# Two-layer hybrid trunk on one core: stores issued by ScalarE, and the modulation product on quarters of TensorE's columns

## Chip, core and metric

The kernel runs on one core of a Trainium2 chip. The metric is the device time of one execution in microseconds. Before the change it was 3992.55 us, the median of 3 runs (3977.74 to 3996.63).

## What is computed

A trunk of two layers over 2304 tokens (256 of context, then 2048 latent) of width 1024, in float32. Of the reference, this matters here:

```python
for i in range(DEPTH):                       # two layers
    sh_l, sc_l, gt_l = ada_modulation(c, w_mod[i], b_mod[i])       # silu(c) @ w_mod + b_mod, split in 3
    sh_c, sc_c, gt_c = ada_modulation(c_ctx, w_mod[i], b_mod[i])
    ml = layer_norm(xl) * (1.0 + sc_l) + sh_l
    mc = layer_norm(xc) * (1.0 + sc_c) + sh_c
    ... = jnp.split(ml @ w_in[i], PROJ_SPLITS, axis=-1)            # one wide projection, three branches
    oa_c, oa_l = gdn_branch(...)     # bidirectional gated DeltaNet, chunks of 64
    ob_c, ob_l = na_branch(...)      # neighbourhood attention
    oc_c, oc_l = gla_branch(...)     # bidirectional gated linear attention
    y_l = concatenate([norm_gate(oa_l), ob_l * silu(z), norm_gate(oc_l)]) @ w_out[i]
    xl = layer_norm(ALPHA * xl + gt_l * y_l) * ln_g[i] + ln_b[i]
```

The modulation product has two rows alone (the conditioning of the latent tokens and of the context) against a 1024 x 3072 matrix in each layer.

## The kernel before

The tokens lie in 18 tiles of 128, and in 6 blocks of 384. The order of every engine's instructions is made when the program is built, by a scheduler that puts whatever is ready first on its engine by priority and by a planned time; the order that results is then fixed, each engine takes its own list in order, and waits on semaphores. All DMAs before are issued by SP, in one list, so an issue that waits holds back all those behind it.

The stages of a layer, with the lines that matter here:

- `stage_mod` (line 90) makes the modulation in parts of 512 columns: parts 0 to 3 are shift and scale, 4 and 5 the gate of the layer's end. For each part it loads the bias `b` (line 98), loads eight 128 x 512 slices `w` of the matrix (line 102), multiplies each by the two columns `e.cc[:, k]` into one PSUM tile `p` of 2 x 512 (line 104), adds the bias (line 105), and transposes the two rows into columns of `modT` (lines 111, 112), or stores them to `GT` (line 107). Layer 0 makes parts 0 to 3 at the very start; parts 4 and 5 of layer 0 and 0 to 3 of layer 1 lie in the first convolution run of layer 0, parts 4 and 5 of layer 1 in that of layer 1. A float32 product shows as two passes in the trace: 96 products are 192 matmuls.
- `stage_p1` (line 161) and `modulate` (line 136) load `x`, normalise it, transpose it (line 153), let ScalarE scale and shift it into `m` (line 156) and store it to `M` in DRAM (line 158). In layer 0's last stage `modulate` is called again for each tile, for layer 1.
- `Dense.block` loads `M` (line 237), splits it into two halves `mm` and stores these to `MS` (line 240); later runs load `MS` (line 234). `Dense.run` multiplies with `w_in` (line 190, the bulk of TensorE's work); its weights are loaded as `raw` (line 220).
- `Gla` consumes the callbacks `cb_q`, `cb_r`, `cb_v` (stores at lines 352, 360, 371) and stores a forward output per tile (`OC`, line 523).
- `Gdn.conv` makes convolutions on VectorE; `head_prep` stores q and k (line 665, last written by VectorE) and `kvt` (line 693, last written by ScalarE) to `KK`. `gates` stores `GR` and `GE` (line 747). `Gdn.step` is the recurrence over 18 tiles in two directions; it stores its output to `OA` (line 1040): the first of the two directions to reach a tile copies it with ScalarE (line 1039), the second loads what is there and adds with VectorE (lines 1035, 1036).
- `Natten.cb_v` stores `Vb` (line 1095). `Out` ends the layer.

Of the kernel before, what the change touches and what calls it, by code (L numbers as in the profile page):

```python
# [89 lines left out]
def stage_mod(e, pool, ps, tag, tt, bufs, w_mod, b_mod, modT, GT, parts, step):  # L90


    nc = e.nc
    w4 = w_mod.rearrange("(k p) n -> p k n", p=128)
    for n in parts:
        s = slice(512 * n, 512 * n + 512)
        b = pool.tile([2, 512], F32, tag="bm", name="b", bufs=2)
        nc.sync.dma_start(b, b_mod[s].partition_broadcast(2))
        p = ps.tile([2, 512], F32, tag=tag, name="p")
        for k in range(0, KD, step):  # L100
            w = pool.tile([128, step, 512], F32, tag="wm", name="w", bufs=bufs)
            nc.sync.dma_start(w, w4[:, k:k + step, s])
            for j in range(step):
                nc.tensor.matmul(p, e.cc[:, k + j], w[:, j], start=k + j == 0, stop=k + j == KD - 1)  # L104
        nc.vector.tensor_tensor(b, b, p, op=ALU.add)
        if n >= 4:
            nc.sync.dma_start(GT[:, 512 * (n - 4):512 * (n - 3)], b)
            continue
        pt = ps.tile([128, 4, 2], F32, tag=tt, name="pt")
        for j in range(4):  # L110
            nc.tensor.transpose(pt[:, j], b[:, j * 128:(j + 1) * 128], e.ident[0:2, 0:2])
        nc.vector.tensor_scalar(modT[:, 4 * n:4 * n + 4], pt, float(n >= 2), None, op0=ALU.add)
# [25 lines left out]
def modulate(e, P, ps, x, mu, r, t, modT, M, xn=None):  # L138
# [19 lines left out]
    nc.sync.dma_start(M[b][:, :, o:o + 128], m)  # L158
# [169 lines left out]
class Gla:  # L328
# [20 lines left out]
    def cb_q(self, P):  # L349
        def f(p, b):  # L350
            self.e.nc.scalar.activation(self.qk0[:, 1], p, AF.Copy, scale=32 ** -0.5)
            self.e.nc.sync.dma_start(self.QK[b], self.qk0)
        return f

    def cb_r(self, P, ps):
        def f(p, b):
            e, nc = self.e, self.e.nc
            r = P.tile([48, BLK], F32, tag="r48", name="r48", bufs=1)
            nc.scalar.copy(r, p)
            nc.sync.dma_start(self.RC[b], r[0:32])  # L360
            pt = ps.tile([128, TPB, 48], F32, tag="dn", name="pt")
            for t in range(TPB):
                nc.tensor.transpose(pt[:, t], r[:, t * 128:(t + 1) * 128], e.ident[0:48, 0:48])
            nc.vector.tensor_copy(e.ab[:, b * TPB:(b + 1) * TPB], pt[:, :, 32:48])
        return f

    def cb_v(self, P):
        def f(p, t):
            v = P.tile([128, 256], F32, tag="bv", name="cv")
            self.e.nc.scalar.copy(v, p[:, 0:256])  # L370
            self.e.nc.sync.dma_start(self.V[t * 128:(t + 1) * 128], v)
# [137 lines left out]
    def chunk(self, c, i, A, E, et, V):  # L509
        e, nc, P, ps = self.e, self.e.nc, self.p, self.ps  # L510
        t0 = i * 128
        if c >= self.first:
# [10 lines left out]
            nc.sync.dma_start(self.OC[c], o1)  # L523
# [52 lines left out]
class Gdn:  # L576
# [84 lines left out]
    def head_prep(self, P, psd, h, b, kq, vb):  # L661
# [31 lines left out]
        nc.sync.dma_start(self.KK[c0:c1, :, h, 2:4].rearrange("c p i t -> p c (i t)"), kvt.rearrange("p c i t -> p c (i t)"))  # L693

    def gates(self, P, ps):
# [34 lines left out]
        for d in range(2):  # L730
# [15 lines left out]
            for x, y in enumerate((self.GR, self.GE)):  # L746
                nc.sync.dma_start(y[d], gr[:, x])
# [230 lines left out]
    def step(self, s, d, c, n):  # L978
# [55 lines left out]
        if c in s.seen:  # L1034
            nc.sync.dma_start(ot, self.OA[c, :, h0:h0 + 2])
            nc.vector.tensor_tensor(ot, ot, po, op=ALU.add)
        else:
            s.seen.add(c)
            nc.scalar.copy(ot, po)
        nc.sync.dma_start(self.OA[c, :, h0:h0 + 2], ot)  # L1040
# [3 lines left out]
class Natten:  # L1044
# [44 lines left out]
    def cb_v(self, P):  # L1089
        nc = self.e.nc  # L1090

        def f(p, t):
            v = P.tile([128, 256], F32, tag="bv", name="bv")
            nc.scalar.copy(v, p[:, 0:256])
            nc.sync.dma_start(self.V[t * 128:(t + 1) * 128], v)
# [313 lines left out]
def layer(e, i, L, layers, xsrc, xdst):  # L1409
# [5 lines left out]
    with ExitStack() as lx:  # L1415
# [8 lines left out]
        if L == 0:  # L1424
            with ExitStack() as c:
# [3 lines left out]
                for n in (range(2), range(2, 4)):  # L1429
                    stage_mod(e, P, ps, "pa", "pm", 11, i["w_mod"][0], i["b_mod"][0], layers[0].modT, GT, n, 1)  # L1430
                    next(p1, None)
# [10 lines left out]
        with ExitStack() as gx:  # L1442
            with ExitStack() as dx:
                psd = pool(dx, "psd", 2, space=PSUM)
                dn = Dense(e, dx, psd, w, M)
                with ExitStack() as r:
# [15 lines left out]
                    with ExitStack() as c:  # L1462
                        ps = pool(c, "psr", 2, space=PSUM)
                        P, W = pool(c, "cv"), pool(c, "wa", side="right")
                        with ExitStack() as c1:
# [4 lines left out]
                            for j, n in ((L, range(4, 6)), (L + 1, range(4))):  # L1470
                                if j < DEPTH:
                                    stage_mod(e, P1, ps, "dn", "dn", 4, i["w_mod"][j], i["b_mod"][j], layers[j].modT, layers[j].GT, n, 1)
# [64 lines left out]
```

## Time and profile before

| | |
|---|---|
| median of 3 runs | 3992.55 us |
| the profiled execution | 3995.01 us, of which the span of instructions is 3992.9 us |
| TensorE busy | 3626.0 us (91%) |
| VectorE, ScalarE, GpSimd busy | 2521.8 us (63%), 1660.0 us (42%), 810.2 us (20%) |
| DMA | 787.57 MB, all but 4.9 MB of it on one queue; 63.6% of the 16 engines' time |
| mean granted TensorE clock | 0.913 of full speed |

Busy time of TensorE is modelled and includes stalls inside a stream, so the table says which engine is used most, not what ends the program last. For that the profile follows a chain back from the last instruction to whatever released each one. Issuing a DMA is not counted as busy time of the engine that issues it; it shows as instructions of a queue (SPq is SP's), with a duration of their own.

### The profile page before, as it was taken

Reading aid. Unit: us, or ns where it says so; the run is one execution under the profiler, and the core shown is the slowest. Engines: PE = TensorE matmul, PEld = TensorE weight load, DVE = VectorE, ACT = ScalarE, POOL = GpSimd, SP = SyncE. Lnnn points to the kernel's source line nnn. Section 1 sums busy time; section 2 is a strip of 40 time slices with the busy share of each in tenths; the row PEclk is TensorE's granted clock in tenths of the full one; section 3 lists DMA queues with packets and bytes.
Section 4 is the critical chain, followed back from the end, with each engine's and each line's share of the span. In section 5 each row is a group of like instructions: output and inputs, shape, how many; then the busy total and the mean of one; then the engine's idle time right before and its main releaser. Section 6 shows DMA issues by size and latency. Waiting matters only on the chain.

```text
span 3992.9 us, 77074 instructions
## 1 busy us (share of the span) xinstructions
PE 3626.0 (91%) x27262; PEld 3113.1 (78%) x27262; DVE 2521.8 (63%) x7471; ACT 1660.0 (42%) x4387; POOL 810.2 (20%) x1182
## 2 busy tenths in 40 slices
PE   7999998899989999897898999999999898989788
PEld 3777787579977888896676778887998788879676
DVE  5465462668975676356875556527798766753587
ACT  4533231335433454446545333213454244545342
POOL 0121111210101332221232211112111132331133
PEclk8988988899999998898898888899999998988899
DMA  9843435876687876666647443268776887775753
GB/s 312 280 147 105 133 112 169 245 232 201 205 276 219 246 229 189 187 196 214 203 132 232 152 147 115 100 210 251 215 232 201 285 228 205 228 217 150 219 160 111
DMA packets 756088, 787.57 MB, mean 197 GB/s; under 512 B 190207, under 2 KB 665207, under 8 KB 755703
## 3 DMA queue, kind: packets, MB, share of 16 engines
q1 hardware_dynamic: 755702, 782.64, 63.6%
q8 instruction: 216, 3.54, 0.4%
q14 instruction: 170, 1.38, 0.1%
HBM read 548.41 MB, written 234.03 MB: 196 GB/s over the span
## 4 chain that ended last, share of the span: by engine, by line
PE 55%; DMA 19%; DVE 16%; ACT 4%; issue 3%; SPq 2%; POOL 0%; DVEq 0%; ACTq 0%; POOLq 0%
PE p L190 29%; DMA mm<-MS 3%; PE p L1245 3%; DMA gb<-GR 2%; PE p L104 2%; DMA kk<-KK 2%; DMA raw<-in_w_in 1%; PE py L190 1%; PE po L1030 1%; PE pk L999 1%; PE pv L1010 1%; DMA oa<-OA 1%; PE pd L1017 1%; PE pt L1236 1%; DVE y L1374 1%
## 5 line engine op out<-in xcount | busy, mean ns | idle before, releaser
L190 PE MATMUL p<-mm,wh 128*128 128x384 f32 (+1 forms) x3648 | 1004.0, 354 | 67.2 <-DMA mm<-MS 21.4
L190 PEld LDWEIGHTS p<-mm,wh 128*128 128x128 f32 (+1 forms) x3648 | 667.8, 192 | 133.7 <-DMA mm<-MS 36.9
L190 PE MATMUL p<-mm,wl 128*128 128x384 f32 (+1 forms) x1824 | 635.1, 350 | 1.8 <-DVE wl L182 1.8
L190 PE MATMUL p<-wh,mm 128*128 128x512 f32 (+1 forms) x1696 | 570.5, 409 | 14.5 <-DMA mm<-MS 4.9
L190 PEld LDWEIGHTS p<-wh,mm 128*128 128x128 f32 x1696 | 329.1, 197 | 92.0 <-DMA mm<-MS 8.4
L649 DVE SCALAR_TENSOR_TENSOR acc<-pre,cw,acc 128x384 f32<-128x384 f32 (+1 forms) x576 | 351.8, 629 | 39.2 <-ACT acc L647 35.8
L190 PEld LDWEIGHTS p<-mm,wl 128*128 128x128 f32 (+1 forms) x1824 | 348.9, 191 | 22.8 <-issue 14.6
L190 PE MATMUL p<-wl,mm 128*128 128x512 f32 (+1 forms) x848 | 341.5, 403 | 4.3 <-DVE wl L182 4.3
L190 PE MATMUL py<-wh,mh 128*128 128x512 f32 x544 | 221.7, 410 | 17.1 <-ACT mh L1360 13.2
L190 PE MATMUL py<-wh,ml 128*128 128x512 f32 x544 | 213.9, 405 | 8.7 <-DVE ml L1361 8.7
L190 PE MATMUL py<-wl,mh 128*128 128x512 f32 x544 | 217.8, 402 | 0.0
L190 PEld LDWEIGHTS p<-wl,mm 128*128 128x128 f32 x848 | 166.5, 196 | 38.5 <-DVE wl L182 4.8
L992 POOL TENSOR_TENSOR kd<-kk,eD 128x256 f32<-128x256 f32 x144 | 90.4, 628 | 476.4 <-DMA kk<-KK 225.6
L1224 ACT ACTIVATE w<-w,mn 128x696 f32<-128x696 f32 (+2 forms) x136 | 112.9, 830 | 143.9 <-DVE mn L1221 142.6
L1383 POOL TENSOR_TENSOR y<-y,g 128x1024 f32<-128x1024 f32 x32 | 77.5, 2423 | 416.0 <-ACT y L1382 416.0
L639 POOL COPY pre<-pre 128x4 f32<-128x4 f32 x120 | 75.0, 627 | 416.4 <-DVE acc L649 244.1
L913 DVE TENSOR_TENSOR tmp<-M 96x30 f32<-96x30 f32 (+4 forms) x360 | 127.1, 353 | 27.7 <-issue 11.3
L1245 PE MATMUL p<-v,wl 120*128 120x64 f32 (+1 forms) x960 | 141.1, 286 | 0.0
L853 DVE SCALAR_TENSOR_TENSOR gb<-gb,Gt,mats 128x128 f32<-128x128 f32 x288 | 86.7, 358 | 83.0 <-DMA gb<-GR 82.8
L1261 DVE SCALAR_TENSOR_TENSOR zt<-zt,p 128x256 f32<-128x256 f32 (+1 forms) x102 | 51.4, 506 | 138.8 <-ACT zt L1260 131.9
L190 PEld LDWEIGHTS py<-wh,mh 128*128 128x128 f32 x544 | 106.4, 196 | 41.4 <-ACT mh L1360 16.1
L914 DVE TENSOR_TENSOR M<-M,tmp 96x30 f32<-96x30 f32 (+4 forms) x360 | 130.4, 362 | 6.1
(307 smaller groups left out, 8021.8 us busy)
## 6 DMA issues: line engine op xcount, KB each, us to landing
mm<-MS SPq DMA_DIRECT2D x384, 384.0 KB
kk<-KK SPq DMA_DIRECT2D x144, 512.0 KB
MS<-mm SPq DMA_DIRECT2D x96, 384.0 KB
raw<-in_w_in SPq DMA_DIRECT2D x104, 256.0 KB
w<-in_w_mod SPq DMA_DIRECT2D x96, 256.0 KB
M<-m SPq DMA_DIRECT2D x36, 512.0 KB
mm<-M SPq DMA_DIRECT2D x96, 192.0 KB
KK<-kq SPq DMA_DIRECT2D x96, 192.0 KB
```

What stands on the lines that cost most here:

```text
L104: nc.tensor.matmul(p, e.cc[:, k + j], w[:, j], start=k + j == 0, stop=k + j == KD - 1)
L190: e.nc.tensor.matmul(p, x(k), y(k), start=n == 0, stop=n == 3 * KD - 1)
L639: nc.gpsimd.tensor_copy(pre[:, 0:4], pre[:, m:m + 4])
L649: nc.vector.scalar_tensor_tensor(acc[:, :n], pre[:, k:k + n], w(kind, k), acc[:, :n], op0=ALU.mult, op1=ALU.add)
L853: nc.vector.scalar_tensor_tensor(E[:, d, h], gb[:, d, h], self.G[:, d, c, h0 + h:h0 + h + 1], e.mats[:, 1 + d], op0=ALU.subtract, op1=ALU.min)
L913: nc.vector.tensor_tensor(tv, col, row, op=ALU.mult)
L914: nc.vector.tensor_tensor(o, o, tv, op=ALU.add)
L992: nc.gpsimd.tensor_tensor(kd, kv[:, :, 0], self.eD[:, d, c, h0:h0 + 2].unsqueeze(2).to_broadcast([128, 2, 128]), op=ALU.mult)
L1224: nc.scalar.activation(w[:, a, 0:256 + nk], w[:, a, 0:256 + nk], AF.Exp, bias=m[:, a:a + 1], scale=-1.0, accum_out=sm[:, a:a + 1])
L1245: nc.tensor.matmul(p[:, a], l, r, start=j == 0, stop=j == len(parts) - 1)
L1261: nc.vector.scalar_tensor_tensor(th[:, :n], th[:, :n], 1.0, z, op0=ALU.add, op1=ALU.mult)
L1383: eng.tensor_tensor(y[:, s], y[:, s], self.g[:, 0, s], op=ALU.mult)
```

## The change

Two edits. **Stores**: where ScalarE is the last to write what a store sends out, the store is issued by ScalarE (`nc.scalar.dma_start`) instead of SP. These are 36 of `M`, 12 of `QKc`, 12 of `RC`, 36 of `Vc`, 34 of `OC`, 48 of `KK<-kvt`, 8 of `GR` and `GE`, 36 of `Vb`, and 68 of the 136 of `OA` (those after the copy): 290 DMAs. **Modulation**: up to four parts are made together. Part i takes partitions 32i and 32i+1 of the PSUM tile, and its product stands on the i-th quarter of the array's columns. One load brings two parts' slices (128 x 1024, 512 KB), so 48 loads take the place of 96; the bias is added part by part, and the transposes take all 128 partitions. `b` is zeroed first, on GpSimd. At the start 6 buffers of 512 KB take the place of 11 of 256 KB, in the convolution runs 2 in place of 4. The first block's `x` and its statistics are now asked for ahead of the modulation.

```diff
-    for n in parts:
-        s = slice(512 * n, 512 * n + 512)
...
-        p = ps.tile([2, 512], F32, tag=tag, name="p")
-        for k in range(0, KD, step):
-            w = pool.tile([128, step, 512], F32, tag="wm", name="w", bufs=bufs)
-            nc.sync.dma_start(w, w4[:, k:k + step, s])
-            for j in range(step):
-                nc.tensor.matmul(p, e.cc[:, k + j], w[:, j], start=k + j == 0, stop=k + j == KD - 1)
-        nc.vector.tensor_tensor(b, b, p, op=ALU.add)
...
+    n0, n = parts[0], len(parts)
+    b = pool.tile([128, 512], F32, tag="bm", name="b", bufs=1)
+    nc.gpsimd.memset(b, 0.0)
+    for i, x in enumerate(parts):
+        nc.sync.dma_start(b[32 * i:32 * i + 2], b_mod[512 * x:512 * x + 512].partition_broadcast(2))
+    p = ps.tile([128, 512], F32, tag=tag, name="p")
+    for k in range(KD):
+        for i0 in range(0, n, 2):
+            w = pool.tile([128, 2, 512], F32, tag="wm", name="w", bufs=bufs)
+            nc.sync.dma_start(w, w4[:, k, 512 * (n0 + i0):512 * (n0 + i0) + 1024].rearrange("p (i c) -> p i c", i=2))
+            for i in range(i0, i0 + 2):
+                nc.tensor.matmul(p[32 * i:32 * i + 2], e.cc[:, k], w[:, i - i0], start=k == 0, stop=k == KD - 1, tile_position=(0, 32 * i))
+    for i in range(n):
+        r = slice(32 * i, 32 * i + 2)
+        nc.vector.tensor_tensor(b[r], b[r], p[r], op=ALU.add)
...
+    for j in range(4):
+        nc.tensor.transpose(pt[:, j], b[:, j * 128:(j + 1) * 128], e.ident)
...
-    nc.sync.dma_start(M[b][:, :, o:o + 128], m)
+    nc.scalar.dma_start(M[b][:, :, o:o + 128], m)
...
-            nc.sync.dma_start(self.OC[c], o1)
+            nc.scalar.dma_start(self.OC[c], o1)
...
-        nc.sync.dma_start(self.KK[c0:c1, :, h, 2:4].rearrange("c p i t -> p c (i t)"), kvt.rearrange("p c i t -> p c (i t)"))
+        nc.scalar.dma_start(self.KK[c0:c1, :, h, 2:4].rearrange("c p i t -> p c (i t)"), kvt.rearrange("p c i t -> p c (i t)"))
...
             nc.vector.tensor_tensor(ot, ot, po, op=ALU.add)
+            nc.sync.dma_start(self.OA[c, :, h0:h0 + 2], ot)
         else:
             s.seen.add(c)
             nc.scalar.copy(ot, po)
-        nc.sync.dma_start(self.OA[c, :, h0:h0 + 2], ot)
+            nc.scalar.dma_start(self.OA[c, :, h0:h0 + 2], ot)
...
-                for n in (range(2), range(2, 4)):
-                    stage_mod(e, P, ps, "pa", "pm", 11, i["w_mod"][0], i["b_mod"][0], layers[0].modT, GT, n, 1)
-                    next(p1, None)
+                next(p1)
+                stage_mod(e, P, ps, "pa", "pm", 6, i["w_mod"][0], i["b_mod"][0], layers[0].modT, GT, range(4))
+                next(p1, None)
...
-                                    stage_mod(e, P1, ps, "dn", "dn", 4, i["w_mod"][j], i["b_mod"][j], layers[j].modT, layers[j].GT, n, 1)
+                                    stage_mod(e, P1, ps, "dn", "dn", 2, i["w_mod"][j], i["b_mod"][j], layers[j].modT, layers[j].GT, n)
```

The same one-word edit as in `modulate` is made in `cb_q`, `cb_r`, both `cb_v` and `gates`. The scheduler makes a new order from this, on every engine. Three places show what it moved. Lines of the new program are 8 higher in its first part (198 is the old 190, 164 the old 156), and 9 higher in the layer's code.

The first is TensorE in the first convolution run of layer 0, where modulation products (`p<-w,cc`) stand among the dense products. Before:

```order
L104 MATMUL p<-w,cc 2x512
L190 MATMUL p<-mm,wl 128x384
L190 MATMUL p<-mm,wh 128x384
L104 MATMUL p<-w,cc 2x512
L190 MATMUL p<-mm,wh 128x384
L190 MATMUL p<-mm,wl 128x384
L190 MATMUL p<-mm,wh 128x384
L104 MATMUL p<-w,cc 2x512
```

And now:

```order
L198 MATMUL p<-mm,wl 128x384
L198 MATMUL p<-mm,wh 128x384 x2
L107 MATMUL p<-w,cc 2x512 x2
L198 MATMUL p<-mm,wl 128x384
L198 MATMUL p<-mm,wh 128x384 x2
L198 MATMUL p<-mm,wl 128x384
L198 MATMUL p<-mm,wh 128x384 x2
L198 MATMUL p<-mm,wl 128x384
L107 MATMUL p<-w,cc 2x512 x2
```

Single products became pairs on two quarters of the columns; the 48 products of this run stand in 22 places in place of 38. At the program's start all 32 stand together, ahead of the first transpose.

The second is SP just after the last modulation load at the start, where the first block of `M` is stored and loaded back. Before:

```order
L158 DMA M_70<-m 1024x1x128
L220 DMA raw<-in_w_in 128x256 x2
L158 DMA M_70<-m 1024x1x128
L167 DMA x<-in_x 128x1024
L220 DMA raw<-in_w_in 128x256 x2
L167 DMA x<-in_x 128x1024
L220 DMA raw<-in_w_in 128x256 x2
L158 DMA M_70<-m 1024x1x128
L167 DMA x<-in_x 128x1024
L220 DMA raw<-in_w_in 128x256 x2
L158 DMA M_71<-m 1024x1x128
L237 DMA mm<-M_70 128x384 x7
```

And now:

```order
L105 DMA w<-in_w_mod 128x1024 x2
L228 DMA raw<-in_w_in 128x256 x9
L175 DMA x<-in_x 128x1024
L228 DMA raw<-in_w_in 128x256 x3
L228 DMA raw<-in_w_in 128x4x128
L175 DMA x<-in_x 128x1024
L228 DMA raw<-in_w_in 128x4x128 x3
L175 DMA x<-in_x 128x1024
L228 DMA raw<-in_w_in 128x4x128 x2
L175 DMA x<-in_x 128x1024
L228 DMA raw<-in_w_in 128x4x128
L245 DMA mm<-M_70 128x384 x8
```

The stores of `M` are gone from SP's list, and the loads that stood between them follow one another.

The third is ScalarE at the same place, as it is now (before, its list held activations and casts alone):

```order
L164 ACTIVATE m<-p,modT_77 128x128 x4
L166 DMA M_70<-m 1024x1x128
L187 CAST wh<-raw 128x256
L164 ACTIVATE m<-p,modT_77 128x128 x4
L187 CAST wh<-raw 128x256
L164 ACTIVATE m<-p,modT_77 128x128
L187 CAST wh<-raw 128x256
L164 ACTIVATE m<-p,modT_77 128x128 x3
L166 DMA M_70<-m 1024x1x128
L187 CAST wh<-raw 128x512
```

A store stands directly behind the last activation of its tile, and the casts and activations of the next tile behind the store.

## Rows read from the trace of the kernel before

**Rows 1.** The page: busy time by engine, and the chain's shares by engine.

```profile
PE 3626.0 (91%) x27262; PEld 3113.1 (78%) x27262; DVE 2521.8 (63%) x7471; ACT 1660.0 (42%) x4387; POOL 810.2 (20%) x1182
...
PE 55%; DMA 19%; DVE 16%; ACT 4%; issue 3%; SPq 2%; POOL 0%; DVEq 0%; ACTq 0%; POOLq 0%
```

**Rows 2.** Chain by line in stretches 0:45, 40:90, 735:870 and 2690:2780.

```profile
by line: PE p L104 47.2%; DMA w<-in_w_mod 34.5%; SPq L1275 4.0%; SPq L1277 2.6%; issue 1.6%; DVE b L105 1.5%; SPq L98 1.4%; DVE lnst L122 1.3%; SPq L83 1.3%; SPq L82 0.9%; SPq L571 0.9%; SPq L569 0.9%; PE pt L111 0.8%
...
by line: DMA M<-m 24.3%; DMA x<-in_x 18.8%; ACT m L156 11.7%; PE p L190 9.7%; DVE lnst L122 8.8%; PE p L104 8.6%; issue 5.7%; ACT mm L179 5.3%; DVE wl L182 1.5%; DVE b L105 1.3%; PE p L153 1.3%; DVE lnmv L123 1.1%; SPq L220 1.0%; PE pt L363
...
by line: PE p L190 50.7%; PE p L104 29.0%; DMA mm<-MS 13.5%; SPq L1118 1.7%; PE pq L670 1.5%; PE p L676 0.9%; PE p L690 0.8%; PE pt L111 0.5%; SPq L102 0.4%; SPq L234 0.4%; issue 0.3%; SPq L98 0.2%
...
by line: DVE acc L649 24.0%; DMA raw<-in_w_in 20.1%; DMA db<-in_dt_bias 6.8%; DMA mm<-MS 6.2%; issue 6.0%; DVE wl L182 5.0%; DVE kq L654 4.0%; ACT wh L179 3.5%; DVE s L712 2.7%; SPq L234 2.6%; ACT acc L647 2.1%; SPq L1118 2.0%; DVE vb L654 
```

**Rows 3.** Windows, line 104 alone: length, PE, PEld, granted clock, DMA share, GB/s.

```profile
0.00:45.00 45.00, 31.38 (x64) 4.85 (x64) 1.00 0.94 307
735.00:870.00 135.00, 47.35 (x96) 4.99 (x96) 1.00 0.89 260
2690.00:2780.00 90.00, 16.68 (x32) 1.81 (x32) 0.98 0.86 254
```

**Rows 4.** Waits of SP's queue: line, releaser: us in total, times, longest.

```profile
SPq L234 <- PE p L190: 179.7, 156, 12.8
...
SPq L693 <- ACT kvt L692: 77.0, 24, 8.2
...
SPq L523 <- ACT kd L529: 43.8, 17, 5.6
...
SPq L523 <- ACT o L522: 40.9, 10, 15.3
...
SPq L352 <- ACT cqk L351: 30.9, 7, 7.9
...
SPq L360 <- ACT r L359: 19.9, 6, 11.1
...
SPq L158 <- ACT m L156: 16.0, 8, 3.3
```

**Rows 5.** Timeline of PE: a modulation product (two passes) between dense ones.

```profile
842.82 1.02 PE L104 MATMUL p<-w,cc 128*2 128x512 f32 x2
843.77 0.62 PE L190 MATMUL p<-mm,wh 128*128 128x384 f32 x2
```

**Rows 6.** Timeline of PE: eight products on quarters of the columns (16 passes).

```profile
552.74 0.51 PE L190 MATMUL p<-mm,wh 128*128 128x384 f32 x2
553.18 0.43 PE L533 MATMUL pS<-v,kd 128*32 128x64 f32 x16
553.54 0.44 PE L190 MATMUL p<-mm,wl 128*128 128x384 f32 x1
```

**Rows 7.** Timeline of DVE: the last part's bias and its write to modT.

```profile
43.92 0.67 DVE L105 TENSOR_TENSOR b<-b,p 2x512 f32<-2x512 f32 x1 [2.06 <-PE p L104]
...
45.73 0.14 DVE L112 TENSOR_SCALAR modT<-pt 128x8 f32<-128x8 f32 x1
```

**Rows 8.** Chain in order of time: two landings of M; who waits for line 158.

```profile
63.36 5.25 DMA M<-m
...
74.27 6.89 DMA M<-m
...
  ACT m L156: 9.4, 8
```

**Rows 9.** Issue durations on SP (ns, min/median/max) at three lines.

```profile
L158 SPq DMA_DIRECT2D M<-m x36: 513/528/1105, 49.5 to 2154.4; - x36
...
L693 SPq DMA_DIRECT2D KK<-kvt x48: 359/366/1673, 794.5 to 3124.0; - x48
...
L1040 SPq DMA_DIRECT2D OA<-o x136: 319/382/1523, 1282.6 to 3745.3; - x136
```

**Rows 10.** Window 45:85, all engines: PE, PEld, DVE, ACT, POOL, clock, DMA.

```profile
45.00:85.00 40.00, 26.34 (x124) 19.61 (x123) 31.10 (x86) 33.04 (x92) 4.83 (x4) 0.66 0.92 302
```

More of the change, by code (lines that the diff above doesn't have):

```diff
@@ L87, in stage_cond, with stage_mod @@
     return cc
-def stage_mod(e, pool, ps, tag, tt, bufs, w_mod, b_mod, modT, GT, parts, step):
+def stage_mod(e, pool, ps, tag, tt, bufs, w_mod, b_mod, modT, GT, parts):
     nc = e.nc
     w4 = w_mod.rearrange("(k p) n -> p k n", p=128)
-    for n in parts:
-        s = slice(512 * n, 512 * n + 512)
-        b = pool.tile([2, 512], F32, tag="bm", name="b", bufs=2)
-        nc.sync.dma_start(b, b_mod[s].partition_broadcast(2))
-        p = ps.tile([2, 512], F32, tag=tag, name="p")
-        for k in range(0, KD, step):
-            w = pool.tile([128, step, 512], F32, tag="wm", name="w", bufs=bufs)
-            nc.sync.dma_start(w, w4[:, k:k + step, s])
-            for j in range(step):
-                nc.tensor.matmul(p, e.cc[:, k + j], w[:, j], start=k + j == 0, stop=k + j == KD - 1)
-        nc.vector.tensor_tensor(b, b, p, op=ALU.add)
[L106 to L112, printed above, removed]
@@ new lines, in stage_mod @@
+    for i in range(n):
+        r = slice(32 * i, 32 * i + 2)
+        nc.vector.tensor_tensor(b[r], b[r], p[r], op=ALU.add)
+    if n0 >= 4:
+        for i in range(n):
+            nc.sync.dma_start(GT[:, 512 * (n0 - 4 + i):512 * (n0 - 3 + i)], b[32 * i:32 * i + 2])
+        return
+    pt = ps.tile([128, 4, 128], F32, tag=tt, name="pt")
+    for j in range(4):
+        nc.tensor.transpose(pt[:, j], b[:, j * 128:(j + 1) * 128], e.ident)
+    for i in range(n):
+        m = modT[:, 4 * (n0 + i):4 * (n0 + i) + 4]
+        nc.vector.tensor_scalar(m, pt[:, :, 32 * i:32 * i + 2], float(n0 + i >= 2), None, op0=ALU.add)
@@ L351, in f @@
             self.e.nc.scalar.activation(self.qk0[:, 1], p, AF.Copy, scale=32 ** -0.5)
-            self.e.nc.sync.dma_start(self.QK[b], self.qk0)
+            self.e.nc.scalar.dma_start(self.QK[b], self.qk0)
         return f
@@ L359, in f @@
             nc.scalar.copy(r, p)
-            nc.sync.dma_start(self.RC[b], r[0:32])
+            nc.scalar.dma_start(self.RC[b], r[0:32])
             pt = ps.tile([128, TPB, 48], F32, tag="dn", name="pt")
@@ L370, in f @@
             self.e.nc.scalar.copy(v, p[:, 0:256])
-            self.e.nc.sync.dma_start(self.V[t * 128:(t + 1) * 128], v)
+            self.e.nc.scalar.dma_start(self.V[t * 128:(t + 1) * 128], v)
         return f
@@ L746, in gates @@
             for x, y in enumerate((self.GR, self.GE)):
-                nc.sync.dma_start(y[d], gr[:, x])
+                nc.scalar.dma_start(y[d], gr[:, x])
     def open(self, ctx):
@@ L1094, in f @@
             nc.scalar.copy(v, p[:, 0:256])
-            nc.sync.dma_start(self.V[t * 128:(t + 1) * 128], v)
+            nc.scalar.dma_start(self.V[t * 128:(t + 1) * 128], v)
         return f
```

## The prediction

> **What bounds the kernel now.** I read the chain of waits first, by engine for the whole span [rows 1] and then by line in the stretches that the change touches [rows 2]; then the windows of line 104 [rows 3], and then SP's own waits [rows 4]. The reader should see in the first that no single engine ends the program. TensorE holds 55% of the chain, transfers hold 19% (759 us of 3992.9), VectorE 16%, ScalarE only 4% (160 us) and SP's queue itself 2% (80 us). In the second, the modulation product is 47.2% of the chain in the first 45 us, with its loads another 34.5%; it is 29.0% in 735 to 870; and in the first of the lines of 2690 to 2780 it does not appear at all: VectorE's convolution and loads are there. In the third, the DMA engines are 0.94, 0.89 and 0.86 busy in these same stretches, so the product lies where transfers are close to being the next bound. In the fourth, SP waits longest for TensorE (179.7 us at line 234 alone), which the change does not touch; the stores that move cost it 77.0 + 43.8 + 40.9 + 30.9 + 19.9 + 16.0 = 228.5 us.
>
> The sum is made against the profiled execution: 3995.0 us, of which 3992.9 are its span. That is 2.5 us over the median of the runs shown.
>
> **The modulation product in layer 0's convolution run.** One product of 2 x 512, which is two passes, takes 0.95 us from its start to that of the dense product behind it [rows 5], so a pass takes 0.48 at most. Do quarters of the columns work side by side in float32? The kernel has such products already: eight of 64 columns, 16 passes [rows 6]. A pass of 64 columns would take an eighth of 0.48, 0.06 us (an estimate from rows 5), and 16 in a line 0.95; but the dense product behind starts 0.36 after the first of them. Four at a time would be 0.24, so they overlap, and some 0.12 us is left for entering and leaving. A pair then costs 0.95 + 0.12, say 1.10, where two singles cost 1.90. The order has 48 products as 24 pairs, most of them alone between dense ones, so quarters 0 and 1 work while 2 and 3 stand empty: 24 x 0.80 = 19 us of TensorE's time. What caps this is the transfers: 0.89 of 135 us is 120 us of DMA work, and the bytes stay the same, so the stretch can shrink by 15 us at most. I take **12 us**, with 0 and 19 as ends.
>
> A rule of the Trainium skill speaks against this edit: TensorEngine Tiling (Array Packing), section Key Properties, says that a change of the tiling mode, not just of the tile, drains TensorE. With 22 changes in this run and 7 in layer 1's, the trace's 0.12 us makes this some 4 us, which the price of a pair holds already; a drain as long as a dense pass would make it no more than twice that.
>
> **The same in layer 1.** 16 products, 16.68 us of busy time [rows 3], would give 8 x 0.80 = 6 us, but the chain of that stretch runs through VectorE and loads. I take **0** (0 to 6).
>
> **At the start.** TensorE's 32 products shrink from 31.38 us to some 8, but the loads stay: 8.4 MB of the matrix. In SP's new order, two more `x` tiles and 0.5 MB more of `raw` stand ahead of its last load, 1.6 MB that take 5 us at the 307 GB/s that the stretch moves [rows 3]. Behind the last product come four bias additions of 0.67 us and four writes to `modT` of 0.14 in place of one each [rows 7]: 2.5 us more. Against that, the `x` tiles are there earlier, and loads of `x` hold 18.8% of the chain from 40 to 90 [rows 2], 9 us, most of which can go. What was TensorE's wait becomes a wait for transfers, and the balance is **0**, between 8 us lost and 8 won. The four clearings of `b` on GpSimd cost nothing: GpSimd is busy 20% [rows 1], and each is needed only when the first bias lands; without that cover it would be under 1 us each (an estimate: the bias addition over the same 512 columns takes 0.67).
>
> **Stores of M on a queue of their own.** In 40 to 90, landings of `M` hold 24.3% of the chain: 5.25 and 6.89 us [rows 8], since ScalarE waits until one of its two `m` buffers is free. Issued by ScalarE they no longer stand behind SP's loads. At worst nothing is won, since the same DMA engines are 0.92 busy [rows 10]; at best half of the 12. I take **4 us**.
>
> **SP freed.** 290 issues at 0.38 us (the median at line 1040, between those of lines 693 and 158 [rows 9]) are 110 us, and with the waits 339 us, 8.5% of SP's time. The lower end is 8.5% of SP's own 80 us on the chain, 7 us. The upper end is that every transfer on the chain starts earlier in that proportion: 8.5% of 759, 64 us. Many loads start late because TensorE frees a buffer late, which stays, so I go low, to the geometric middle: **21 us**. The new wait in place of the old is just that one, on PE at line 234.
>
> Against this stands the Trainium skill's DMA: Bandwidth & Descriptors, section Issuing engines are not separate DMA queues: whoever issues, the transfers end on the same 16 engines, and only the sequencer's issue time is saved. By that rule this part is worth the issue time's share alone, 2 us, and that of `M` nothing, which is the second rival below.
>
> **ScalarE loaded.** It now issues these 290: 110 us more on an engine that is busy 1660 us. Queued behind each is ScalarE's next work: the PSUM copies that TensorE waits for in the convolution runs, the next tile's scaling in the first stage, the `v` of the recurrence. About a tenth of ScalarE's busy time is on the chain (160 of 1660), so a tenth of the new time should be: **11 us lost**, between 0 and all of the 110. [...]
>
> **The sum:** 12 + 0 + 0 + 4 + 21 - 11 = 26 us less, 3969 on the profiled execution's scale, and **3967 us** on that of the median.
>
> **Rivals.**
>
> First, *SP was the brake*. For it: 339 us leave its list, and the scheduler, planning with two queues, can put loads earlier. Against it: the chain gives the queue 2%. The upper ends, 19 + 6 + 8 + 6 + 64 - 11 = 92 us less: 3901 us.
>
> Second, *the change does not reach the end*: the product's place is taken by its own loads, two thirds of what TensorE saves at the start shows as a wait for `w`, and the stores were hidden under waits for TensorE anyway. For it: DMA shares of 0.86 to 0.94 where the product lies, and SP's longest wait. Also here belongs the case that quarters do not work side by side for passes of 512 columns, which [rows 6] speak against. Between 0 and 12 us less: about 3986 us.
>
> Third, on the other side, *ScalarE becomes late*. One mechanism: a store's issue stands in its list ahead of a copy or scaling that TensorE or VectorE awaits, and every later one shifts. It decides as soon as more than 37 of the 110 us reach the end (the gains of 12, 4 and 21), one issue in three. At two in three it is 73 lost against 37 won: 4028 us. For it: the stores stand directly behind the producer, so the issue also waits for that to be written; ScalarE is 83% busy in the first stage. Against it: ScalarE is busy 42% over the span, and just 4% of the chain.
>
> **How the numbers follow.** The forecast (3935 to 3985) has a chance of 0.42, the first rival 0.13, no effect 0.30, ScalarE late 0.15. The range that should hold the time is 3912 to 4022: it takes in all of the forecast and of no effect, most of the first rival's gains short of its upper end, and ScalarE's lateness up to nearly two in three. 0.5%, some 20 us, is about what a measurement of this kernel can tell from no change. Below 3972.6 lie three quarters of the forecast's chance and all of the first rival's: 0.45. Within it the rest of the forecast and nearly all of no effect: 0.38. Slower: 0.17, ScalarE late and a little of no effect, because some of every engine's order is new.
>
> **What would show it.** Right: line 107 at half of line 104's busy time in the first convolution run, with its pairs overlapping; the DMA share there at 0.93 or more; at the start a chain of `w` loads where the product was; SP's waits for ScalarE at the moved lines gone, and those for TensorE at line 242 (the old 234) up; ScalarE's chain share at 4 to 6%. Wrong: a stretch from 735 on that is shorter by 19 us or not at all; ScalarE's share at 8% or more, or issue durations on its queue at over 1 us; TensorE's longest waits going to ScalarE's copies.

## The result, and the profile after

The change is slower: 4015.98 us (median of 20 executions, 3990.3 to 4039.19) against 3995.14 us (20 executions, 3977.74 to 4007.34), a ratio of 1.0054, 95% interval 1.0032 to 1.0076. That is 21 us more, where 26 less were forecast. A second set of executions of the same program gave 1.007 (1.004 to 1.0099). The execution that was profiled, 3990.66 us, is nearly the fastest of the 20; in its trace the chain of waits can be followed over only half of the span, so shares of the chain are read from the profile of the second set (4010.78 us). Of the runs below, that with `KK` alone was profiled in a slower state of the chip (4121.18 us at a granted clock of 0.804), so its waits are not compared.

The page of the changed kernel, engines and queues:

```profile
PE 3560.0 (89%) x27238; PEld 3086.9 (77%) x27238; DVE 2494.5 (63%) x7471; ACT 1660.2 (42%) x4387; POOL 817.4 (20%) x1186
...
q1 hardware_dynamic: 664118, 716.46, 58.7%
q10 hardware_dynamic: 84672, 66.18, 5.1%
```

The page of the second profile of the same program, the chain's shares:

```profile
PE 55%; DMA 17%; DVE 15%; ACT 5%; issue 3%; SPq 2%; POOL 1%; ACTq 0%; DVEq 0%; POOLq 0%
```

Against [rows 1]: TensorE's busy time fell by 66 us (50 in the second profile, 3575.6 us), 66 MB moved to a queue of ScalarE's (q10), and the chain's shares hardly changed. Nothing here looks slower, and the program is. By the prediction's own signs (ScalarE at 4 to 6% of the chain) it should have been right; of the others, the DMA share from 735 to 870 us reached 0.92 in both profiles, short of its 0.93, and the chain at the start cannot be followed in either.

Windows of line 107 (the old 104) alone, columns as in [rows 3]:

```profile
0.00:45.00 45.00, 18.91 (x62) 1.52 (x64) 0.92 0.95 321
740.00:885.00 145.00, 25.51 (x96) 2.33 (x96) 0.98 0.91 271
2690.00:2780.00 90.00, 8.05 (x32) 0.84 (x32) 0.97 0.86 253
```

The timeline of TensorE, a pair on quarters (four passes) and the dense product behind it:

```profile
795.32 1.03 PE L107 MATMUL p<-w,cc 128*2 128x512 f32 x4
796.32 0.62 PE L198 MATMUL p<-mm,wh 128*128 128x384 f32 x2
```

The product's busy time is halved, 47.35 us to 25.51 in layer 0's convolution run and 16.68 to 8.05 in layer 1's. Two quarters work side by side: four passes take the 1.00 us from 795.32 to 796.32, where two passes took 0.95 in [rows 5]. From the start of a pair to that of the instruction behind it, 26 pairs of this trace have a median of 0.957 us, 43 single products of the kernel before 0.950.

Issue durations on ScalarE's queue (ns, min/median/max) at lines 166, 701 and 1049, the old 158, 693 and 1040, and SP's longest wait:

```profile
L166 ACTq DMA_DIRECT2D M<-m x36: 520/521/576, 55.1 to 2156.0; - x36
...
L701 ACTq DMA_DIRECT2D KK<-kvt x48: 366/366/426, 785.3 to 3125.3; - x48
...
L1049 ACTq DMA_DIRECT2D OA<-o x68: 325/326/390, 1281.1 to 3652.4; - x68
...
SPq L242 <- PE p L198: 212.2, 150, 14.0
```

The issues cost ScalarE what [rows 9] said, 110 us over the 290, and none is long. SP's wait for TensorE rose from 179.7 us to 212.2, as expected.

TensorE's timeline at the start:

```profile
14.85 7.45 PE L107 MATMUL p<-w,cc 128*2 128x512 f32 x24 [14.85 <-DVE lnst L130]
27.39 3.20 PE L107 MATMUL p<-w,cc 128*2 128x512 f32 x8 [5.09 <-DMA w<-in_w_mod]
...
48.83 1.09 PE L117 MATMUL pt<-ident,b 128*128 128x128 f32 x4 [3.04 <-DVE b L110]
```

The product begins at 14.85 us (9.42 before) because three `x` tiles and all biases are loaded ahead of the matrix, and 3.04 us of bias additions stand behind it. The first `m` is finished at 52.0 us, not 46.1, and the first dense product ends at 82.8, not 72.3. At the end of the first stage 4.4 us of this are left (0.7 in the second profile).

The landings of `M`, which the prediction wanted halved, were no shorter. Who waited for line 166, in the first profile and in the second (before, 9.4 us, [rows 8]):

```profile
  ACT m L164: 9.5, 4
```

```profile
  ACT m L164: 15.4, 5
```

What did move is in no single large row. Added up over all rows of the view of TensorE's waits, TensorE waited 98.6 us for ScalarE before, and 115.3 and 117.9 in the two profiles after; VectorE waited 587.5 us for ScalarE before, and 639.8 and 639.9 after. TensorE's waits for VectorE rose most, from 166.3 us to 208.3 and 216.4, while those for transfers fell from 78.2 to 70.6 and 65.5. So what TensorE saved in busy time came back as waits.

### The profile page after: what moved, and what is told of

Its sections match the earlier page's. It is cut to its first block, busy times and chain, and to the rows that moved or that the text cites. A ratio compares the mean times of both kernels' runs of the same rounds, so it can differ in the third digit from the quotient of the medians.

```text
span 3988.9 us, 76787 instructions
## 1 busy us (share of the span) xinstructions
PE 3560.0 (89%) x27238; PEld 3086.9 (77%) x27238; DVE 2494.5 (63%) x7471; ACT 1660.2 (42%) x4387; POOL 817.4 (20%) x1186
## 4 chain that ended last, share of the span: by engine, by line
PE 26%; DMA 10%; DVE 9%; ACT 3%; issue 2%; SPq 1%; POOL 1%; DVEq 0%; ACTq 0%; POOLq 0%
PE p L198 13%; DMA mm<-MS 2%; PE py L198 2%; PE p L1254 1%; DMA raw<-in_w_in 1%; DMA OA<-o 1%; DVE mix L1360 1%; DMA oa<-OA 1%; DVE mix L1359 1%; DVE y L1383 1%; PE pv L1018 1%; PE pd L1025 1%; PE pA L494 1%; DMA kh<-Kb 1%; DMA mm<-M 1%
## 5 line engine op out<-in xcount | busy, mean ns | idle before, releaser
L190 DVE TENSOR_TENSOR wl<-raw,wh 128x512 fp32r<-128x512 f32 (+3 forms) x144 | 92.6, 659 | 74.0 <-ACT wh L187 72.9
L187 ACT CAST wh<-raw 128x512 fp32r<-128x512 f32 (+3 forms) x144 | 76.3, 552 | 138.2 <-DMA raw<-in_w_in 116.4
```

What stands on the lines that cost most here:

```text
L187: eng_hi.copy(hi, src)
L190: eng_lo.tensor_tensor(lo, src, hi.bitcast(F32), op=ALU.subtract)
```

## The experiments

Three theories. **A**, ScalarE late: issuing delays what TensorE and VectorE await from ScalarE. **B**, order: the scheduler made a new order for all engines, and that is what costs. **C**, the clock: the granted clock is lower (median over the executions 0.906, before 0.915). In the first four expectations, "rival theory C" is something else: that the stores are neutral and the product on quarters loses.

### The parts, each alone

The change again; before with only the nine store lines changed; the change with its stores back on SP; and before with only the convolution runs' product on quarters (`stage_mod4` is the new `stage_mod`). One line of nine stands for the stores:

```diff
-    nc.sync.dma_start(M[b][:, :, o:o + 128], m)
+    nc.scalar.dma_start(M[b][:, :, o:o + 128], m)
...
-    stage_mod(e, P1, ps, "dn", "dn", 4, i["w_mod"][j], i["b_mod"][j], layers[j].modT, layers[j].GT, n, 1)
+    stage_mod4(e, P1, ps, "dn", "dn", 2, i["w_mod"][j], i["b_mod"][j], layers[j].modT, layers[j].GT, n)
```

> The changed kernel once more, beside its parts and on the same chip. Its first profiled execution (3991 us) was the fastest of 20, so a second profile is wanted beside the one in hand. Theory A (issues make ScalarE late): ratio to the kernel before 1.003 to 1.008. Theory B (the new order alone, any part gives about the same): the same ratio. Expected of the profile: the first convolution run of layer 0 shorter by 13 us as in the first profile, the first dense product at 82 to 84 us in place of 72.

> The kernel before with the 290 stores issued by ScalarE, the modulation as before. Theory A (ScalarE late): 15 to 35 us slower than before, ratio 1.004 to 1.009. Rival theory C (stores neutral, the modulation loses at the start and in waits for its two buffers): 0.998 to 1.002.

> The changed kernel with all stores on SP again, so the modulation edit alone, at the start and in the convolution runs. Theory A: 5 to 15 us faster than before (13 won in the convolution run of layer 0, 6 lost at the start), ratio 0.996 to 0.999. Rival theory C: 10 to 25 us slower, ratio 1.003 to 1.006.

> The kernel before with the new modulation in the convolution runs alone; at the start the old one, stores on SP. Theory A: 10 to 20 us faster, ratio 0.995 to 0.998, and 6 to 10 us faster than with the new start too. Rival theory C: 0 to 10 us slower.

| run | us | ratio (95%) |
|---|---|---|
| the change again | 4024.84 | 1.0070 (1.0040 to 1.0099) |
| stores alone | 4009.06 | 1.0040 (1.0014 to 1.0065) |
| modulation alone | 4001.85 | 1.0021 (0.9997 to 1.0044) |
| modulation in the convolution runs alone | 3989.03 | 0.9981 (0.9955 to 1.0007) |

The stores cost 16 us where 14 were to be won. The modulation alone, 1.0021, fits neither theory's range. The product on quarters in the convolution runs shows the gain in its own place: from the reciprocal in `gates` (VectorE, layer 0) to the end of the first `kvt`, 78.9 us for 86.6 (73.3 in the whole change). But each of these kernels also has a new order on every engine: with the stores alone, layer 1's last stage, which has no moved store, grew from 202 to 230 us. So the parts had to be measured with the order held.

### Queue and order apart

The kernel is planned twice: once as one variant, to get each engine's order, and then as another, tied to that order by edges that only order the issues of one engine. This is f1, planned with the stores on SP (`False`) and built with them on ScalarE (`True`); f2 has the two the other way round:

```diff
+            for seq in list_.values():
+                seq = [k for k in seq if was[k] == engines[k]]
+                for p, q in zip(seq, seq[1:]):
+                    tc.add_manual_dep(ins[q], ins[p].name, mybir.DependencyInfo(mybir.DependencyClass.NoSync, mybir.DependencyReason.DATA), reason="order")
...
+    order = build(plan, src, False, None)
...
+    build(nc, src, True, order)
```

> The 290 stores are issued by ScalarE, as in the run with the stores alone (ratio 1.004), but every other instruction stands on its engine in exactly the order of the kernel before; only the stores' own places in ScalarE's list are new. Theory A (ScalarE late: the 108 us of issue time that ScalarE now pays delay what TensorE waits for): as slow as with the new order, ratio 1.003 to 1.006, ScalarE more often the releaser of TensorE. Theory B (the new order of the other 34,900 instructions costs the time, whoever issues): ratio 0.995 to 1.001, mean granted clock back at 0.914 to 0.916, where the run with the stores alone had 0.910. My own forecast of the stores' worth (14 us less) would be 0.9965.

> The opposite corner: all stores are issued by SP as before, but every other instruction stands in the order that the scheduler made for the stores on ScalarE. Theory A: ratio 0.999 to 1.001, since ScalarE issues nothing. Theory B: ratio 1.003 to 1.006 and a mean granted clock near 0.910, as in the run with the stores alone. If both matter, this and the run with the old order share the 16 us between them.

| order | stores on | ratio (95%) | TensorE's waits for ScalarE, for transfers | VectorE's for ScalarE |
|---|---|---|---|---|
| before's | SP (before) | 1 | 98.6, 78.2 us | 587.5 us |
| before's | ScalarE (f1) | 1.0032 (1.0012 to 1.0053) | 120.4, 62.5 | 613.8 |
| made for ScalarE | SP (f2) | 1.0054 (1.0032 to 1.0076) | 85.1, 81.9 | 554.7 |
| made for ScalarE | ScalarE (e2) | 1.0040 (1.0014 to 1.0065) | 105.8, 59.4 | 584.1 |

Both theories hold, and neither alone. In either order the queue does the same to the waits: 21 to 22 us more for ScalarE, 16 to 23 us less for transfers. These are the two effects that the prediction had. At before's order the queue costs 13 us; at the new order it costs nothing that can be told. And the new order alone, with not one instruction or queue changed, costs 21 us. Its largest piece is layer 1's last stage, in both kernels that have this order. Windows over that stage, all engines, of before, of e2 and of f2 (length, then PE, PEld, DVE, ACT, POOL, granted clock, DMA):

```profile
3781.00:3983.00 202.00, 183.18 (x840) 147.38 (x838) 171.39 (x476) 75.20 (x278) 74.10 (x30) 0.99 0.43 141
```

```profile
3764.00:3994.00 230.00, 199.25 (x838) 156.73 (x836) 178.23 (x475) 75.15 (x280) 72.12 (x30) 0.92 0.38 122
```

```profile
3763.00:3993.00 230.00, 199.19 (x844) 156.92 (x843) 179.98 (x480) 76.80 (x287) 71.95 (x30) 0.93 0.38 124
```

The same work takes 28 us longer, TensorE is idle for 31 us instead of 19, and the granted clock is 0.92 and 0.93 instead of 0.99. No run rebuilt before in its own order with these edges, to show that they cost nothing; the nearest is the run with `OA` alone below, 1.0008 (0.9988 to 1.0027).

### Which stores

ScalarE's timeline in f1 (before's order; its line numbers are 7 higher than before's) shows what a store in its list can do, at a store of `KK` and at one of `OA`:

```profile
1122.24 0.88 ACT L699 ACTIVATE kvt<-p,inv 128x128 f32<-128x128 f32 x3 [0.29 <-DVE inv L694]
1132.08 0.37 ACTq L700 DMA_DIRECT2D KK<-kvt  x1
1132.49 0.31 ACT L687 ACTIVATE jk<-kvt 128x128 f32<-128x128 f32 x1 [9.36 <-DMA KK<-kq]
...
1309.27 0.37 ACT L1047 COPY o<-po 128x256 f32<-128x256 f32 x1 [4.14 <-PE po L1039]
1318.40 0.33 ACTq L1048 DMA_DIRECT2D OA<-o  x1
1318.89 0.37 ACT L1047 COPY o<-po 128x256 f32<-128x256 f32 x1 [9.26 <-DMA gbs<-GE]
```

and TensorE's, just behind the first:

```profile
1136.61 0.69 PE L683 MATMUL p<-ident,kq 128*128 128x128 f32 x2 [7.55 <-DVE ss L679]
```

The producer `kvt` is finished at 1123.1. The issue comes at 1132.08 and takes 0.37 us: ScalarE stood still for 9 us, because the *store* waited for another transfer to land, `KK<-kq`, which SP had issued. At 1318.40 the profile names a load of `GE`, which has nothing to do with `OA`. ScalarE's list of instructions, with what each waits for, shows such a wait for 247 of the change's 290 stores: one of eight counters of transfers (DMAHW0 to DMAHW7) beside the producer's own. In all 247 it is the counter on which the store's own landing will be counted, so the store waits for the transfer that was given the same counter before it, whatever tensor that was:

```
L701 DMA KK<-kvt 128x3x256 [waits DMAHW1_49,Activation_49]
```

On SP the stores carried such waits too. There they held back other issues; in ScalarE's list they hold back ScalarE: `jk`, with it `nv` on VectorE and `ss` behind that, and then TensorE, for 7.55 us. Added up over the stores, where ScalarE stood more than 0.06 us between its last instruction and the issue: 104.7 us in f1, of which 35.2 before 10 stores of `KK` and 40.6 before 16 of `OA`; 114.4 and 112.8 in the two profiles of the change. So the stores were split, in before's order: 138 on ScalarE without `M`, `KK` and `OA`; only these 152; `KK` alone; `OA` alone. In these four runs the modulation product's own instructions were left out of the held order. With the 138, 39 of its 96 products stand in other places than before, with the 152 and with `KK` 22, with `OA` none; TensorE's waits from 735 to 880 us, in the first convolution run, are 0.7 us (138) and 2.6 us (152), 1.5 us before.

```diff
+def QUEUE(nc, kind):
+    return nc.scalar if kind in ON_ACT.split() else nc.sync
...
-            nc.sync.dma_start(self.OC[c], o1)
+            QUEUE(nc, "OC").dma_start(self.OC[c], o1)
```

> No modulation change; old order; of the 290 stores only 138 go to ScalarE: those of M, KK and OA (36 + 48 + 68), behind which ScalarE's next work follows within 0.5 us in the median, stay on SP. Theory A, refined (an issue costs only where ScalarE has work right behind it): TensorE's waits for ScalarE return from 120 us to about 100 and the ratio to 0.998 to 1.000, against 1.0032 with all 290. If it is the number of issues, not their place, that counts: about half of the loss, 1.001 to 1.002. If SP's freeing is worth anything by itself, this is the run that is faster than before.

> The complement of the run with 138 stores: only the 152 of M, KK and OA are issued by ScalarE (64 us of issue time), the rest by SP, every other instruction in the order of the kernel before. Refined theory A (an issue costs where ScalarE has work right behind it): all of the loss and more, ratio 1.004 to 1.006, TensorE's waits for ScalarE at 115 us or more. If the two groups do not add (SP's queue is what counts, and any mixture of queues is worse or better by itself): 1.000 to 1.002.

> Only the 48 stores of KK (behind kvt in the convolutions) are issued by ScalarE, in the old order. In the runs with all stores on ScalarE TensorE waited 5 to 6 us for kvt instead of 1 to 2, in both orders. If KK holds the largest part of the loss: 1.002 to 1.004; if it holds what that one row shows (5 us): 1.001; if it is OA or M: 0.999 to 1.0005.

> Only the 68 first stores of OA (the recurrence's outputs) are issued by ScalarE, in the old order: 22 us of issue time between the copies of o, v and X that TensorE's chain of the recurrence waits for. If they hold the largest part of the loss: 1.002 to 1.004, with TensorE's waits for v and o up by 9 us as in the run with all stores. If M and KK hold it: 0.998 to 1.0005.

| on ScalarE, before's order | ratio (95%) | TensorE's waits for ScalarE | ScalarE stood before stores |
|---|---|---|---|
| all 290 (f1) | 1.0032 (1.0012 to 1.0053) | 120.4 us | 104.7 us |
| `M`, `KK`, `OA`: 152 (h1) | 1.0051 (1.0030 to 1.0073) | 124.3 | 88.4 |
| the other 138 (g4) | 0.9979 (0.9959 to 0.9999) | 96.7 | 25.2 |
| `KK`: 48 (h2) | 1.0022 (0.9997 to 1.0047) | | |
| `OA`: 68 (h3) | 1.0008 (0.9988 to 1.0027) | 111.4 | 33.5 us |

Two rows of VectorE's waits, in before, f1, h1 and g4 in turn (f1's line numbers are 7 higher than before's, those of h1 and g4 47):

```profile
DVE nv L682 <- ACT jk L680: 15.8, 17, 1.8
DVE X L858 <- ACT gb L855: 6.1, 9, 0.8
```

```profile
DVE nv L689 <- ACT jk L687: 25.4, 16, 9.5
DVE X L865 <- ACT gb L862: 16.9, 12, 6.0
```

```profile
DVE nv L729 <- ACT jk L727: 27.8, 17, 8.0
DVE X L905 <- ACT gb L902: 15.3, 13, 4.5
```

```profile
DVE nv L729 <- ACT jk L727: 15.3, 17, 1.7
DVE X L905 <- ACT gb L902: 7.1, 9, 1.1
```

The 152 stores hold all of the loss, some 20 us, and the other 138 gain 8. The longest single wait goes from 1.8 us to 9.5 and 8.0 and back to 1.7, with those stores. `KK` is the largest part, about 9 us; `OA` 3; what is left for `M` is about 8, though these three are no larger than their intervals. The 152 pay 61 us of issue time and 88 us of standing, the 138 pay 46 and 25. Standing, not issuing, is what separates the two groups in the traces; no run changed the one without the other. Within the 152 it does not order the losses: in h1 ScalarE stood 12.5 us before `M`, 36.4 before `KK` and 39.5 before `OA`, where 8, 9 and 3 us were lost. So that the standing is the cause is argued from the traces; that these stores on ScalarE are is shown.

### The modulation in before's order

The product on quarters in the convolution runs; the same with the new start; the whole change; and the first with three buffers for `w`. Everything outside the product stands in before's order. The last differs from the first by:

```diff
-    modulation(e, stage_mod4, P1, ps, "dn", "dn", 2, i["w_mod"][j], i["b_mod"][j], layers[j].modT, layers[j].GT, n)
+    modulation(e, stage_mod4, P1, ps, "dn", "dn", 3, i["w_mod"][j], i["b_mod"][j], layers[j].modT, layers[j].GT, n)
```

> Only the product on quarters in the convolution runs (48 + 16 products); stores, start and the order of every instruction outside the product as in the kernel before. If the modulation's saving is real and the rest of the 4 us that the run without a fixed order showed was its new order: the stretch from the gates to the first kvt shrinks from 86.6 us to 73 to 79, and the ratio is 0.995 to 0.998 (my forecast was 12 us, 0.997). If the saving is given back behind it (the convolutions wait for transfers or VectorE anyway): ratio 0.999 to 1.001 with that stretch shorter all the same.

> As the run before it in this list, and the new start too: x tiles first, then the product of four quarters. If the start is what it costs: the first m at 51 to 52 us instead of 46, the first dense product 8 us late, and the ratio 0.002 to 0.003 above the run without the new start. If the 13 to 16 us that separated these two kernels under free orders were the order's: the ratio is the same within 0.001, the 8 us being caught up by the end of the first stage.

> The whole change, with every instruction outside the modulation product in the order of the kernel before. The change with its own order had 1.0054 and 1.007. If order is a large part of that (theory B): 0.998 to 1.002. If the parts themselves are slow (ScalarE late by 13 us, start by 8, product -10): 1.002 to 1.005.

> The product on quarters in the convolution runs alone, old order, with three buffers of 512 KB for the matrix instead of two (the kernel before has four of 256 KB). With two, TensorE waited 11.6 us for these loads between 735 and 880 us, where the kernel before waits for none, and the ratio was 1.0029. If these waits are what eats the saving: they fall below 4 us and the ratio to 0.998 to 1.000. If the transfers themselves are the limit there (DMA engines about 0.9 busy): the wait moves to mm or stays, and the ratio stays at 1.001 to 1.003.

| before's order | us | ratio (95%) | gates to first `kvt` (before 86.6) |
|---|---|---|---|
| convolution runs' product (g1) | 4003.99 | 1.0029 (1.0009 to 1.0050) | 85.7 us |
| and the start (g2) | 3996.76 | 1.0007 (0.9981 to 1.0032) | 86.1 |
| and the 290 stores (g3) | 4016.33 | 1.0057 (1.0028 to 1.0086) | 86.0 |
| g1 with three buffers (h4) | 4006.72 | 1.0026 (1.0004 to 1.0048) | 91.1 |

TensorE's waits from 735 to 880 us, in g1 and in h4; before it waited only 1.5 us there, and for `mm`:

```profile
PE p L146 <- DMA w<-in_w_mod: 11.6, 8, 3.0
PE p L237 <- DMA mm<-MS: 2.3, 2, 1.4
```

```profile
PE p L237 <- DMA mm<-MS: 8.2, 5, 3.4
PE p L146 <- DMA w<-in_w_mod: 4.6, 5, 1.5
```

In before's order the pairs stand between the same dense products as the singles did, and TensorE waits for their loads: the time saved becomes a wait for `w`. With a third buffer that wait moves to `mm`, and the kernel is no faster: TensorE waits for transfers in this stretch with either number of buffers. Whether the 16 DMA engines set that (0.87 and 0.84 busy there, 0.85 before) or SP's list, which in g1 waits 20.8 us at line 712 for VectorE's `kq` (16.2 us before), no run separates. The granted clock in these 145 us is 0.95 and 0.92, before 1.00. My expectation that the saving would stay in this order failed. So did the one that the new start costs: it does not, 0.0022 less than without it. The 13 us between the two kernels under free orders I put down to the orders, though their intervals overlap. And the whole change costs the same in before's order as in its own, so its own order is no excuse for it: the parts in this order, +12, -9 and the stores' +13, make 16 of its 23 us, with intervals that hold the rest.

### A version that is faster

The modulation alone, but with the weights traced ahead of the `x` tiles (run twice); this with the 138 stores in a free order; and with the 138 stores in the order of the kernel without them:

```diff
-                next(p1)
                 stage_mod(e, P, ps, "pa", "pm", 6, i["w_mod"][0], i["b_mod"][0], layers[0].modT, GT, range(4))
+                next(p1)
                 next(p1, None)
```

> The modulation alone (stores on SP), with the quarters' product at the start too, but traced ahead of the first x tiles, so that the loads of the modulation matrix lead SP's list. In the run with the modulation alone the first dense product came 8 us late and the ratio was 1.0021; with the old start it was 0.9981. If the loads in front of the matrix cost the start, the first m comes at 46 us and the first dense product at 72 us as before, and the ratio is 0.996 to 0.999. If the quarters' own form costs it (all four quarters end only with the last load; four bias additions and one wide transpose then stand in a line), the first m stays at 50 us or later and the ratio at 1.001 to 1.003. By theory C (TensorE's granted clock falls to its lower level while the product waits for loads) the time at the lower level in the first 85 us stays at 40 us where the kernel before has 23 us.

> The same program as the run with the weights first: 0.995 to 0.998 if its 0.9966 was the program's, 0.999 to 1.002 if it was that set of executions'.

> Both modulations on quarters with the weights traced first, and the 138 stores of QK, RC, V, OC, GR and GE issued by ScalarE while those of M, KK and OA stay on SP; the scheduler's own order. If the two gains are properties of the edits, they add: ratio 0.993 to 0.996. If the gain of the weights-first run was its order's, the new order decides: anything from 0.996 to 1.004, with TensorE's waits for ScalarE still at 85 to 108 us, since no tight store is on it.

> Both modulations on quarters with the weights traced first, every instruction in the order that the scheduler made for that kernel (0.9966 twice), and the same 138 stores moved to ScalarE on top of it. If the order alone spoiled the joined run (1.011): 0.993 to 0.9975, layer 1's last stage at 209 us and not 223. If the two edits get in each other's way: 1.000 or more, with the same order.

| run | us | ratio (95%) |
|---|---|---|
| weights first (f3) | 3983.99 | 0.9966 (0.9936 to 0.9996) |
| again (k2) | 3983.10 | 0.9966 (0.9941 to 0.9991) |
| and 138 stores, free order (k1) | 4040.22 | 1.0110 (1.0076 to 1.0143) |
| and 138 stores, k2's order (m1) | 3977.29 | 0.9942 (0.9921 to 0.9964) |

Weights first is 14 us faster, but not by the way I had expected: its first `m` is finished at 52.8 us and the first dense product ends at 80.4, nearly as late as with the `x` tiles first (82.8, and 81.6 in the second profile). Its gain lies further on, and I put it down to its order; no run shows it. k1 and m1 have the same instructions on the same queues, and only their order differs: 4040 and 3977 us, 63 us apart; k1 fell outside both ranges that I had given. With the order kept, the 138 stores come to 10 us less, as in before's order (8), though the intervals of m1 and k2 overlap. m1 is faster than before by 23 us and than the change by more.

## Why the prediction was wrong

The time lies inside the stated range of 3912 to 4022 by the range's breadth alone; the direction was wrong. In before's order, the product's 12 us won came out as 12 lost, the start's 0 as 9 won, and the stores' 14 won (4 + 21 - 11) as 13 lost.

- **The modulation product, 12 us less.** The price was too careful and the conclusion too hopeful. A pair takes 0.957 us, not 1.10. The stretch became 8 to 13 us shorter where the scheduler was free to rearrange it, and 1 us in before's order; the whole program gained 8 us in the one, with an interval that takes in 0, and lost 12 in the other. What took the saving in before's order was named in the second rival: the product's place is taken by its own loads (11.6 us of waits for `w`). The Trainium skill, TensorEngine Tiling (Array Packing), section Key Properties, has a change of the tiling mode drain TensorE; the 0.007 us between 0.957 and 0.950 is all that this trace leaves for it.
- **Layer 1's, 0,** cannot be told from the other runs' product. **At the start, 0,** with 8 either way, held as far as can be told: 9 us won in before's order, with an interval that takes in 0, although the first dense product began 5.8 us late there. Its working did not: TensorE's busy time at the start fell to 18.9 us, not to some 8.
- **Stores of M, 4 us less:** ScalarE's waits for the landings stayed at 9.5 us, or rose to 15.4, where half was to go. What the other runs leave for these stores, by subtraction, is some 8 us lost; no run had them alone.
- **SP freed, 21 us less.** The effect is real: TensorE's waits for transfers fell by 16 to 23 us. Where it stands without the stores that hurt, it is worth 8 us (138 stores), net of what their issues cost ScalarE. The Trainium skill, DMA: Bandwidth & Descriptors, section Issuing engines are not separate DMA queues, lets a second issuer save the issue time alone. The estimate worked out from that, 2 us for all 290, is less than was measured for these 138, but their interval, 0 to 16 us, does not rule it out.
- **ScalarE loaded, 11 us more:** this is the step that failed most. I priced the stores by their issue durations (110 us, a tenth on the chain) and took SP's waits at their lines, 228.5 us, as gone. But a store takes its waits along, not for its producer alone: 247 of the 290 wait for a counter of transfers too. In [rows 4] that part did not show: at line 693 SP waited 77.0 us for ScalarE's `kvt`, and 2.4 us for a transfer. Probably SP came late to these stores, when the transfer had landed; no run tests that. ScalarE comes at once, and stood 105 to 114 us before its stores, as much again as the issues cost. M, KK and OA lose 20 us net, not a part of 11. This is the third rival, with the right place and a wrong price for its cause.
- **The signs** were badly chosen. ScalarE's share of the chain (5%) and the issue durations (below 0.6 us) stayed where I had called it right. The loss sits in the waits of TensorE and VectorE for ScalarE, added up over many rows.
- **Order** was a half sentence ("some of every engine's order is new"). It is worth as much as any term: 21 us between two kernels with equal instructions and queues (before and f2), 63 between two others (k1 and m1).

## What to carry to other kernels

A DMA that is moved from SP to a compute engine takes all its waits into that engine's list. Before moving it, list what it waits for besides its producer, and move only stores behind which that engine has nothing that others await. Where a scheduler orders the whole program anew for each edit, hold the order while parts are measured; otherwise the order's own tens of microseconds are read as the edit's.

## What was not expected of the hardware

- Two float32 products of two rows on two quarters of the columns cost TensorE the time of one: 0.957 us for four passes, 0.950 for two.
- Executions of one program differ by over 1%, and the granted clock goes along: before's 31 executions in the first series run from 3967.26 us at 0.918 to 4017.66 at 0.910, and over them 0.01 of the clock goes with some 35 us (19 to 30 in the later series). The change's lower median (0.906 against 0.915) would by that be about all of its loss or more. But the weights-first kernel has the same 0.906 and is faster than before, although its first 85 us have 54.6 us at the lower of the two levels, half of full speed (27.3 before). And the stores' loss in before's order comes without it: f1 has 0.913 and h1 0.913, where before has 0.914, and they are 13 and 20 us slower. So for the stores theory C fails; for the order and the product it is not settled: the time at the lower level may be a cause or only a trace of where TensorE waited, and no run varied it alone.
